# The way back from the experts: pairs of 64-column float32 products from one unsplit buffer

## The chip, the cores and the metric

The kernel runs on one core of a Trainium2 chip. The metric is the time of one execution on the device in microseconds (us); the kernel before takes 1039.68 us, the median of 3 runs (1038.59 to 1040.19).

## The reference

A decoder trunk of two layers on 512 tokens of 1024 features, all in float32. Each layer is a mixer and then a hierarchical mixture of experts, both with a residual and a layer norm. The mixture is what the change touches:

```python
def hier_moe(x, rg_w, rg_b, re_w, re_b, w1, w3, w2):
    ...   # top-1 of 4 groups, then top-2 of the group's 8 experts: gates (tokens, 32), zero for experts not chosen
    def expert(acc, params):
        w1e, w3e, w2e, ge = params
        h = jax.nn.silu(xf @ w1e) * (xf @ w3e)
        return acc + ge[:, None] * (h @ w2e), None
    out, _ = lax.scan(expert, jnp.zeros_like(xf), (w1, w3, w2, gates.T.astype(x.dtype)))
    return out.reshape(B, S, D)
...
    x = layer_norm(ALPHA * x + mixer(x))      # per layer, with its gain and offset
    x = layer_norm(ALPHA * x + hier_moe(x))
```

So each token's row of the result is its own row plus the gated outputs of two experts.

## The kernel before

The program has four parts in a row: mixer of layer 0, its mixture, mixer of layer 1, its mixture (`trunk_kernel`). The rows of `x` lie in four tiles of 128 tokens with 1024 features each (`x_63` to `x_66` in the lists below).

**The mixture** (`moe`) never computes an expert for a token that did not choose it. The routing gives each expert a list of places. Fourteen groups of 128 places are worked off one after the other: the first four hold two experts of 64 places each, the other ten are put together of blocks of 32 places, so that a group is one, two, three or four experts wide (tile sizes 128, 64, 32 columns in the shapes of the profile). For a group, GpSimd gathers the 128 rows from memory (`xg`), TensorE transposes them (`pt`) and ScalarE brings them back with gain and offset (`xt`), TensorE multiplies with w1 and w3 (`hidden`, into `ph`, line L1835), ScalarE and VectorE make silu, gate and product (`hs`), TensorE transposes that (`pth`), ScalarE copies it (`hT`), and TensorE multiplies with w2 in two halves of 512 features (`outputs`, into `py`, L1857). Each expert of a group takes its own columns of the array, and writes its own partitions of the bank.

**The way back.** `outputs` does not keep the group's result as it is: `split` (L287, L288) has ScalarE round it to float32r (`yh`) and VectorE make the float32r rest (`yl`). `places` has VectorE make a matrix P of zeros and ones that tells for each of the 128 places which of the 512 tokens it belongs to. `combine` then, for one tile of 128 tokens and one half of the features, multiplies 128 columns of P with `yh` and with `yl`, both into one bank (`pcm`, L1872), and VectorE adds the bank to `x` (L1874). Eight such sums bring a group home. They are not made at once: they go to a list (`todo`), and during the next group `some` takes them from it at fixed places: two before the fourth and two before the last of the eight steps of `hidden`, one between the two halves of the transposes, one after them, and one before each half of `outputs`.

**The order** in the mixture is that of the program: within it no scheduler moves anything. Each engine works down its own list, and waits where an operand is not there.

**The last group.** In layer 0 the sums of the last group are made in the mixer that follows (`sums` in `mixer1`): there `join` normalises each tile of tokens (VectorE: mean; ScalarE: squares with their sum; GpSimd: power -1/2; VectorE: scale), `turn` transposes it in quarters of the features, and `dense` multiplies. In layer 1 the last two groups are summed in `finish`, which also normalises and writes the result. Both lie behind a branch for blocks that found no place (`tc.If`), which is not taken here.

**The planner** (`Flow`). Both mixers are streams of steps; `Flow.run` puts them into one order before the program runs, taking for each step when its operands are expected and when its engine is free. `Flow.cost` has the prices: of a matmul of n columns n/2330 us where the left side is not float32, n/600 us where it is and the product is not narrow (128 rows deep is not). `Flow.clocked` doubles that where the array is expected to be slow. The planner takes the products of TensorE one after the other. The order that comes out is fixed in the program.

Of the kernel before, what the change touches and what calls it, by code (L numbers as in the profile page):

```python
# [30 lines left out]
class Flow:  # L31
    """Puts the work of several streams into one order. A stream is a generator that yields, before each step, the engine
    the step starts on and the tiles it needs; the order follows from when those are expected to be there, with
    `streams` in order of priority."""
# [83 lines left out]
    def enter(self, tensor):  # L118
        """the place of a tile in its ring"""
        ring = self.rings.setdefault(tensor.tag, [])  # L120
        if tensor.name not in self.place:
            self.place[tensor.name] = len(ring)
            ring.append(tensor.name)
        return self.place[tensor.name], ring
# [3 lines left out]
    def is_warm(self, k):  # L128
        """the array runs at its full clock in a tick that follows one with enough columns"""
        return k > 0 and self.columns.get(k - 1, 0.0) >= self.enough  # L130
# [24 lines left out]
    def take(self, pool, shape, name, bufs):  # L155
        """a tile of a ring, once the reads of the one before it there have been put in order"""
        taken = self.rooms.setdefault(name, [])
        while len(taken) >= bufs and not taken[-bufs]:
            yield None
        t = pool.tile(shape, F32, name=name, bufs=bufs)  # L160
        self.enter(t.tensor)
        taken.append(False)
        self.version += 1
        return t, (taken, len(taken) - 1)
# [5 lines left out]
    def run(self, streams):  # L170
# [3 lines left out]
        while state:  # L174
            best, moved = None, False
            # an array that rests is slow: work that fills it first, where there was too little
# [32 lines left out]
def run_streams(main, fill, ratio):  # L209
    """Emit several streams of work in one order. A step of a stream yields (tensor-engine time, time from its end until  # L210
    the stream's next step can start), or "blocked" where another stream has to go first. `main` streams go in order of
    priority; `fill` streams take the time in which they wait, and at least `ratio` of theirs."""
# [37 lines left out]
class Kernel:  # L250
# [12 lines left out]
    def setup(self):  # L263
# [12 lines left out]
        # x^T of a mixer; after its projections what the mixture of experts starts with  # L276
        self.xp = self.ctx.enter_context(self.tc.tile_pool(name="xp", bufs=1))
        self.dp = self.ctx.enter_context(self.tc.tile_pool(name="dp", bufs=1, space=DRAM))

    def x_room(self, order=(0, 1, 2, 3)):  # L280
        """x^T: [high, low parts][half of the features]"""
# [9 lines left out]
    def mixer0(self):  # L291
        """Feature-major tiles hold two heads on the partitions and 512 tokens; token-major ones hold two chunks of 64 tokens
        (p = 0, 1) on the partitions, and 4 pairs of chunks, heads and features along them. With L the part of a chunk's
        own tokens, T = (I - L)^-1, W = T a and u0 = T (a k^T v), the state after a chunk is
        decay (S + b^T (W S + u0) + k^T v), so all but the product with S is made for every chunk at once."""
# [6 lines left out]
        with ctx:  # L302
# [19 lines left out]
            # weights in the order of their use  # L322
            # (numbers: columns of the input projection; else rows of the output projection: whose, which, a half of the columns)
# [18 lines left out]
            def halve(raw, eng, e):  # L342
                """the float32r part of weights, and the rest"""
# [22 lines left out]
            # lnx_g for tokens on partitions  # L366
# [55 lines left out]
            def unit(parts):  # L422
                """one bank's worth of products: parts [(left, right)] for every 128 rows"""
# [16 lines left out]
            def dense():  # L440
                """the input projection and the output projection"""
# [20 lines left out]
            def evacuate():  # L462
                n, begun = -1, set()
                for job in jobs:
# [17 lines left out]
                    if ti >= 14:  # L482
                        # u, after zeros for the windows
# [25 lines left out]
            def product(needs, shape, f, e):  # L509
                """a bank with f's products, as soon as engine e can read it"""  # L510
# [9 lines left out]
            def head_sums(src):  # L520
                """sums over the features of each head, token-major"""
# [80 lines left out]
            def within(ps, lhsT, rhs):  # L602
                """products of token-major tiles, chunk by chunk"""
# [4 lines left out]
            def across(ps, lhsT, rhs, out="p", **kw):  # L608
                """products over one half of the partitions that go to either half, a bank for every half"""
# [17 lines left out]
            def solve():  # L627
                """T, transposed, and what follows from it"""
                for i in range(4):
# [56 lines left out]
                    # W and u0  # L686
# [14 lines left out]
                    # what the state is multiplied with, for the next state and for y  # L701
# [12 lines left out]
                    # what chunks add to the state  # L714
# [19 lines left out]
            def side():  # L734
                """what the inverse doesn't wait for: tiles turned token-major, and products with k"""
# [64 lines left out]
            def states():  # L800
                """chunk after chunk: the state, and y"""
                for i in range(4):
# [8 lines left out]
                    # one accumulation for a bank: the first matmul of each half clears it  # L811
# [24 lines left out]
                    # (a state made after the products above goes first, so that these don't run beside them)  # L836
# [12 lines left out]
            def heads():  # L849
                """head norm, bonus and gate"""  # L850
# [87 lines left out]
    def mixer1(self):  # L938
# [5 lines left out]
        with ctx:  # L944
# [12 lines left out]
            # weights in the order of their use: (what, which), [rows / 128, columns]  # L957
# [68 lines left out]
            def sums():  # L1026
                """the last of the sums of the mixture before; the sums of every tile go to its layer norm"""
                for t in range(NT):
                    total[t] = bp.tile([128, 2], F32, name=f"jsum{t}", bufs=1)
                    for h in range(2):  # L1030
                        fs = slice(512 * h, 512 * h + 512)
                        ps, room = yield from bank(pp, [512], "pp")
                        ops = [(P, y) for P, ys in late for y in ys]
                        for n, (P, y) in enumerate(ops):
                            yield "PE", (P, y)
                            mm(ps, P[:, 128 * t:128 * t + 128], y[:, fs], start=n == 0, stop=n == len(ops) - 1)
# [6 lines left out]
            def join(t):  # L1043
                """layer norm of the mixture before; x gets its gain and offset later"""
# [13 lines left out]
            def turn(h, g):  # L1058
                """x^T of a quarter of the features of two tiles of tokens, with gain and offset"""
# [343 lines left out]
    def moments(self, pool, x):  # L1403
        """mean, and the reciprocal of the standard deviation"""
# [17 lines left out]
    def start(self, L, flow, pool, turn, sums):  # L1422
        """streams for the start of the mixture: what it takes from memory (once the room of x^T is free), then for every
        tile of tokens the logits and the normalised rows. The router takes x as it is: gain, offset, mean and deviation
        go into its weights, and into what becomes of its sums."""
# [96 lines left out]
    def moe(self, L, last):  # L1522
        """The first experts have 64 places each, two to a group of 128, and their weights are there before the routing is
        known. The others follow in the order of their tokens, places as `limits` has it: a block of 32, and one more for each
        limit their rank is below. What doesn't fit goes to further blocks of 32."""
# [6 lines left out]
        # of every group: whose columns  # L1532
# [18 lines left out]
        with ctx:  # L1551
# [31 lines left out]
            def load(p, known, to=32):  # L1583
                """weights in the order of their use, as far as there is room after the group p"""
# [41 lines left out]
            # routing  # L1626
# [9 lines left out]
            def ranked(src, n, tag):  # L1636
                """how many of the n are ahead: greater, or as great and earlier"""
# [7 lines left out]
            def gated(to, engine):  # L1645
                """weights that are to come behind what the engine does now"""
# [22 lines left out]
            # place of every assignment in its expert's list  # L1669
# [10 lines left out]
            # of the first experts, which are a group: which assignments are theirs, and the tokens  # L1680
# [15 lines left out]
            def chosen(dst, src, n=32):  # L1696
                """of every assignment its expert's entry"""
# [24 lines left out]
            def tokens(name, tab, n):  # L1722
                """the token of every slot, for the gather (out of bounds where there is none) and as a number"""
# [18 lines left out]
            for h in range(2):  # L1742
                # of the first group the halves of the features by themselves
# [8 lines left out]
            # gates, in three parts that bfloat16 holds  # L1752
# [39 lines left out]
            # ranks of the other experts by how many tokens they have, and who has which  # L1792
# [18 lines left out]
            def columns(xrows, xt=None, halves=(0, 1), both=False):  # L1811
                """x^T of 128 slots"""
# [16 lines left out]
            def hidden(xt, ws, gate, beside=(), now=False):  # L1829
                """gate silu(x w1) (x w3), 128 slots shared by some experts"""  # L1830
# [19 lines left out]
            def outputs(hT, ws, y=None):  # L1850
                yh, yl = y or [bp.tile([128, D], F32R, name=n, bufs=3) for n in ("yh", "yl")]
                for half in range(2):
# [5 lines left out]
                    self.split(yh[:, h], yl[:, h], ps)  # L1858
                return yh, yl

            def places(tok, P=None):
                if P is None:
                    P = bp.tile([128, S], F32R, name="P", bufs=3)
# [3 lines left out]
            def combine(parts, t, half, scale, total=None, room=None):  # L1867
                """x <- scale x + the rows of ys, each at its token; its sum"""
                ps = (room or pr).tile([128, 512], F32, name="pcm", tag="py" if room else "pr")
                ops = [(P, y) for P, ys in parts for y in ys]  # L1870
                for n, (P, y) in enumerate(ops):
# [324 lines left out]
```

## Time and profile before

| | |
|---|---|
| median of 3 runs | 1039.68 us (1038.59 to 1040.19) |
| profiled execution, first to last instruction (its span; the page has no other time of it) | 1034.8 us |
| TensorE matmuls (PE) busy | 914.6 us, 88% |
| VectorE (DVE) busy | 734.7 us, 71% |
| ScalarE (ACT) busy | 339.5 us, 33% |
| GpSimd (POOL) busy | 327.5 us, 32% |
| mean granted clock of TensorE | 0.933 of full speed |

An engine's time is that between start and end of its instructions. Matmuls overlap: the next starts before the one ahead has drained, so the durations of single matmuls add up to more than the time they take, and the distance from start to start is what one costs in a row. A float32 matmul is two records on TensorE, a float32r matmul one. The experts' matmuls lie between about 337 and 509 us and between 836 and 1020 us of the span.

### The profile page before, as it was taken

Reading aid. Unit: us, or ns where it says so; the run is one execution under the profiler, and the core shown is the slowest. Engines: PE = TensorE matmul, PEld = TensorE weight load, DVE = VectorE, ACT = ScalarE, POOL = GpSimd, SP = SyncE. Lnnn points to the kernel's source line nnn. Section 1 sums busy time; section 2 is a strip of 40 time slices with the busy share of each in tenths; the row PEclk is TensorE's granted clock in tenths of the full one; section 3 lists DMA queues with packets and bytes.
Section 4 is the critical chain, followed back from the end, with each engine's and each line's share of the span. In section 5 each row is a group of like instructions: output and inputs, shape, how many; then the busy total and the mean of one; then the engine's idle time right before and its main releaser. Section 6 shows DMA issues by size and latency. Waiting matters only on the chain. (4 is left out here: it accounts for less than half of the span.)

```text
span 1034.8 us, 18665 instructions
## 1 busy us (share of the span) xinstructions
PE 914.6 (88%) x7364; PEld 644.3 (62%) x7364; DVE 734.7 (71%) x1527; ACT 339.5 (33%) x690; POOL 327.5 (32%) x298
## 2 busy tenths in 40 slices
PE   6999999999995599999879589779999748999993
PEld 5777777777775255545368568778878624545542
DVE  3565868576777977776676999994733698767666
ACT  3543242433214233433353012212502333433333
POOL 2120414135303810100169446663422281100003
PEclk9999999999997799999989789988888969999997
DMA  7210101011176859788152121221325165976742
GB/s 216 82 43 22 43 24 41 24 43 60 43 280 221 307 225 359 274 345 334 42 161 76 47 81 42 82 82 41 116 102 214 62 246 227 347 282 247 306 197 83
DMA packets 60012, 156.97 MB, mean 152 GB/s; under 512 B 5153, under 2 KB 40097, under 8 KB 51728
## 3 DMA queue, kind: packets, MB, share of 16 engines
q1 hardware_dynamic: 54256, 141.79, 37.4%
q0 software_dynamic: 4512, 9.74, 3.0%
q10 hardware_dynamic: 1152, 4.19, 1.0%
q8 instruction: 60, 0.98, 0.4%
q14 instruction: 32, 0.26, 0.1%
HBM read 155.71 MB, written 6.29 MB: 157 GB/s over the span
## 5 line engine op out<-in xcount | busy, mean ns | idle before, releaser
L1874 DVE SCALAR_TENSOR_TENSOR x<-x,pcm 128x512 f32<-128x512 f32 x210 | 137.0, 683 | 54.5 <-PE pcm L1872 54.2
L57 PE MATMUL pp<-x,wh 128*128 128x512 f32 x480 | 163.5, 423 | 6.4 <-DVE u L57 5.1
L57 PE MATMUL pp<-wh,x 128*128 128x256 f32 (+1 forms) x544 | 139.2, 342 | 23.3 <-DVE u L57 11.4
L57 DVE SCALAR_TENSOR_TENSOR acc<-u,cw,acc 128x512 f32<-128x512 f32 x120 | 127.8, 1120 | 0.7
L57 ACT CAST wh<-wr 128x512 fp32r<-128x512 f32 (+1 forms) x82 | 61.8, 776 | 192.5 <-PE pp L57 129.0
L57 PEld LDWEIGHTS pp<-wh,x 128*128 128x128 f32 x544 | 100.2, 209 | 34.6 <-DVE u L57 11.6
L1835 PE MATMUL ph<-we,xt 128*64 128x256 f32 (+1 forms) x928 | 116.8, 389 | 0.0
L57 PEld LDWEIGHTS pp<-x,wh 128*128 128x128 f32 x480 | 85.9, 195 | 29.0 <-issue 6.2
L1872 PE MATMUL pcm<-yh,P 128*128 128x512 f32 x216 | 99.2, 459 | 3.0 <-DVEq L2043 2.3
L57 PE MATMUL pp<-x,wl 128*128 128x512 f32 x240 | 96.3, 401 | 0.0
L57 POOL TENSOR_TENSOR wl<-wr,wh 128x1024 fp32r<-128x1024 f32 x28 | 83.3, 2988 | 34.5 <-ACT wh L57 34.5
L57 PE MATMUL pp<-wl,x 128*128 128x256 f32 (+1 forms) x272 | 91.1, 335 | 0.0
L1872 PE MATMUL pcm<-yl,P 128*128 128x512 f32 x216 | 85.8, 397 | 5.1 <-DVE yl L288 5.1
L1824 ACT ACTIVATE xt<-pt,x 128x128 f32<-128x128 f32 x224 | 84.8, 471 | 15.6 <-PE pt L1818 15.6
L1835 PEld LDWEIGHTS ph<-we,xt 128*64 128x64 f32 (+1 forms) x928 | 56.8, 129 | 47.1 <-issue 31.7
L1738 POOL DMA_INDIRECT xg<-xd,imx x20 | 19.9, 993 | 191.9 <-PE pt L1818 147.3
L1872 PEld LDWEIGHTS pcm<-yh,P 128*128 128x128 f32 x216 | 40.6, 188 | 52.0 <-DVE x L1874 28.7
L57 DVE SCALAR_TENSOR_TENSOR x<-x,pp 128x512 f32<-128x512 f32 x64 | 43.6, 685 | 39.6 <-PE pp L57 39.5
L1857 PE MATMUL py<-we,hT 128*64 128x512 f32 (+1 forms) x232 | 62.8, 628 | 0.4 <-ACT hT L1847 0.4
L288 DVE TENSOR_TENSOR yl<-py,yh 128x512 fp32r<-128x512 f32 x54 | 37.1, 691 | 34.3 <-ACT yh L287 34.3
L1839 ACT ACTIVATE hs<-ph 128x128 f32<-128x128 f32 x28 | 7.8, 277 | 160.0 <-PE ph L1835 160.0
L57 PEld LDWEIGHTS pp<-wl,x 128*128 128x128 f32 x272 | 57.4, 211 | 2.8
(427 smaller groups left out, 1657.7 us busy)
## 6 DMA issues: line engine op xcount, KB each, us to landing
we<-in_c_experts_dram SPq DMA_DIRECT2D x56, 1536.0 KB, 9.5
wr<-in_ev_w_in_dram SPq DMA_DIRECT2D x18, 512.0 KB, 3.9
x<-in_c_experts_dram SPq DMA_DIRECT2D x8, 1024.0 KB, 6.1
wr<-in_od_w_in_dram SPq DMA_DIRECT2D x7, 1024.0 KB, 5.1
wr<-in_ev_w_out_dram SPq DMA_DIRECT2D x8, 512.0 KB, 3.7
x<-in_c_experts_dram SPq DMA_DIRECT2D x8, 512.0 KB, 4.2
xd<-x ACTq DMA_DIRECT2D x8, 512.0 KB, 4.1
wr<-in_od_w_in_dram SPq DMA_DIRECT2D x8, 512.0 KB, 5.7
```

The costliest lines, as they stand in the source:

```text
L57: r = f(*args, **kw)
L288: (eng or nc.vector).tensor_tensor(lo, src, hi.bitcast(F32), op=OP.subtract)
L1738: G.indirect_dma_start(out=xg[n % NG], out_offset=None, in_=xd, in_offset=bass.IndirectOffsetOnAxis(ap=idx, axis=0), bounds_check=S - 1, o ...
L1824: A.activation(xt[:, kk], ps[:, k], AF.Identity, scale=gc[:, kk:kk + 1], bias=bc[:, kk:kk + 1])
L1835: mm(hp[r], xt[:, k, r], w[0][:, k], start=k == 0, stop=k == KT - 1)
L1839: A.activation(hs, hp[:, 0], AF.Silu)
L1857: mm(ps[r], hT[:, r], w[1][:, h], start=True, stop=True)
L1872: mm(ps, P[:, 128 * t:128 * t + 128], y[:, 512 * half:512 * half + 512], start=n == 0, stop=n == len(ops) - 1)
L1874: V.scalar_tensor_tensor(xs, xs, scale, ps, op0=OP.mult, op1=OP.add, accum_out=total)
```

## The change

`outputs` keeps the group's result in one float32 buffer `y`, by the same copy of ScalarE; VectorE's part of the split is gone. P is float32. A new function `paired` makes of one product two, each with 64 of the 128 columns of P, into the two halves of the bank; `combine` and `sums` call it once per group where they called the plain product twice. The scratch tile of `finish` takes the new buffer's room. Comments and docstrings are dropped as well, and lines shift by some six.

```diff
+    @staticmethod
+    def paired(mm, out, lhsT, rhs, **kw):
+
+        for c in (slice(0, 64), slice(64, 128)):
+            mm(out[c], lhsT[:, c], rhs, **kw)
...
                         ps, room = yield from bank(pp, [512], "pp")
-                        ops = [(P, y) for P, ys in late for y in ys]
-                        for n, (P, y) in enumerate(ops):
+                        for n, (P, y) in enumerate(late):
                             yield "PE", (P, y)
-                            mm(ps, P[:, 128 * t:128 * t + 128], y[:, fs], start=n == 0, stop=n == len(ops) - 1)
+                            self.paired(mm, ps, P[:, 128 * t:128 * t + 128], y[:, fs], start=n == 0, stop=n == len(late) - 1)
...
             def outputs(hT, ws, y=None):
-                yh, yl = y or [bp.tile([128, D], F32R, name=n, bufs=3) for n in ("yh", "yl")]
+                if y is None:
+                    y = bp.tile([128, D], F32, name="y", bufs=3)
                 for half in range(2):
...
-                    self.split(yh[:, h], yl[:, h], ps)
-                return yh, yl
+                    A.copy(y[:, h], ps)
+                return y
 
             def places(tok, P=None):
                 if P is None:
-                    P = bp.tile([128, S], F32R, name="P", bufs=3)
+                    P = bp.tile([128, S], F32, name="P", bufs=3)
...
-                ops = [(P, y) for P, ys in parts for y in ys]
-                for n, (P, y) in enumerate(ops):
-                    mm(ps, P[:, 128 * t:128 * t + 128], y[:, 512 * half:512 * half + 512], start=n == 0, stop=n == len(ops) - 1)
+                for n, (P, y) in enumerate(parts):
+                    self.paired(mm, ps, P[:, 128 * t:128 * t + 128], y[:, 512 * half:512 * half + 512], start=n == 0,
+                                stop=n == len(parts) - 1)
...
-                    y = self.xp.tile([128, 2, D], F32R, name="x1")
-                    y = y[:, 0], y[:, 1]
-                    P = self.xp.tile([128, 4, S], F32R, name="x2")[:, 0]
+
+                    y = self.xp.tile([128, 2, D], F32, name="x1")[:, 0]
+                    P = self.xp.tile([128, 4, S], F32, name="x2")[:, 0]
...
-                junk = bp.tile([128, D], F32R, name="yl", bufs=3)
+                junk = bp.tile([128, D], F32, name="y", bufs=3)
```

**In a group of two experts** TensorE's list keeps its places and changes what stands in them. Its rows between the last step of `hidden` and the second half of `outputs` are before:

```order
L1835 MATMUL ph<-we,xt 64x256 x2
L1818 MATMUL pt<-ident,xg_3880 128x128 x4
L1872 MATMUL pcm<-yh,P 128x512
L1872 MATMUL pcm<-yl,P 128x512
L1845 MATMUL pth<-ident,hs 128x128
L1818 MATMUL pt<-ident,xg_3880 128x128 x4
L1872 MATMUL pcm<-yh,P 128x512
L1872 MATMUL pcm<-yl,P 128x512
L1872 MATMUL pcm<-yh,P 128x512
L1872 MATMUL pcm<-yl,P 128x512
L1857 MATMUL py<-we,hT 64x512 x2
```

and now:

```order
L1840 MATMUL ph<-we,xt 64x256 x2
L1823 MATMUL pt<-ident,xg_3880 128x128 x4
L284 MATMUL pcm<-y,P 64x512 x2
L1850 MATMUL pth<-ident,hs 128x128
L1823 MATMUL pt<-ident,xg_3880 128x128 x4
L284 MATMUL pcm<-y,P 64x512 x4
L1863 MATMUL py<-we,hT 64x512 x2
L284 MATMUL pcm<-y,P 64x512 x2
```

Each pair of 128-column products (`yh`, `yl`) has become a pair of 64-column products of `y`; a row with x4 is two sums.

**At the entry to the second mixer** the planner puts the work into another order. On VectorE the sums of the four tiles (`jsum`), their means (`jnm`) and their normalisations (which read `jrs`) stood so before:

```order
L57 SCALAR_TENSOR_TENSOR x_63,jsum_6050<-x_63,pp 128x512 x2
L57 SCALAR_TENSOR_TENSOR jnm_6068<-jsum_6050,mean 128x1
L57 SCALAR_TENSOR_TENSOR x_64,jsum_6066<-x_64,pp 128x512 x2
L57 SCALAR_TENSOR_TENSOR x_65,jsum_6080<-x_65,pp 128x512
L57 SCALAR_TENSOR_TENSOR jnm_6082<-jsum_6066,mean 128x1
L57 SCALAR_TENSOR_TENSOR x_65,jsum_6080<-x_65,pp 128x512
L57 SCALAR_TENSOR_TENSOR x_66,jsum_6097<-x_66,pp 128x512
L57 SCALAR_TENSOR_TENSOR jnm_6099<-jsum_6080,mean 128x1
L57 SCALAR_TENSOR_TENSOR x_66,jsum_6097<-x_66,pp 128x512
L57 SCALAR_TENSOR_TENSOR jnm_6111<-jsum_6097,mean 128x1
L57 TENSOR_SCALAR x_63<-x_63,jnm_6068,jrs_6070 128x1024
L57 TENSOR_SCALAR x_64<-x_64,jnm_6082,jrs_6084 128x1024
```

and now:

```order
L57 SCALAR_TENSOR_TENSOR x_63,jsum_6006<-x_63,pp 128x512 x2
L57 SCALAR_TENSOR_TENSOR jnm_6028<-jsum_6006,mean 128x1
L57 TENSOR_SCALAR x_63<-x_63,jnm_6028,jrs_6030 128x1024
L57 SCALAR_TENSOR_TENSOR x_64,jsum_6026<-x_64,pp 128x512 x2
L57 SCALAR_TENSOR_TENSOR jnm_6045<-jsum_6026,mean 128x1
L57 TENSOR_SCALAR x_64<-x_64,jnm_6045,jrs_6047 128x1024
L57 SCALAR_TENSOR_TENSOR x_65,jsum_6043<-x_65,pp 128x512 x2
L57 SCALAR_TENSOR_TENSOR jnm_6071<-jsum_6043,mean 128x1
L57 TENSOR_SCALAR x_65<-x_65,jnm_6071,jrs_6073 128x1024
L57 TENSOR_TENSOR x_5990<-xf,x_5988 128x2x256
L57 SCALAR_TENSOR_TENSOR x_66,jsum_6069<-x_66,pp 128x512 x2
L57 SCALAR_TENSOR_TENSOR jnm_6095<-jsum_6069,mean 128x1
```

The normalisation of a tile, which waits for GpSimd's `jrs`, has moved ahead of the sums of the next tile.

On TensorE, at the end of the transposes of the third and fourth tile of tokens (`x_65`, `x_66`), with the kernel of the convolution (`cwr`) and the first products of the projection, there stood before:

```order
L57 MATMUL pt<-ident,x_65 128x128 x2
L57 MATMUL pt<-ident,x_66 128x128 x2
L57 MATMUL ps<-ident,x_65 128x128 x2
L57 MATMUL ps<-ident,x_66 128x128 x2
L57 MATMUL pt<-ident,cwr 128x31 x4
L57 MATMUL pp<-wh,x_6032 128x256
L57 MATMUL pp<-wl,x_6032 128x256
L57 MATMUL pp<-wh,x_6034 128x256
```

and now:

```order
L57 MATMUL pt<-ident,x_66 128x128 x2
L57 MATMUL ps<-ident,x_66 128x128 x2
L57 MATMUL pt<-ident,cwr 128x31 x4
L57 MATMUL pp<-wh,x_5988 128x256
L57 MATMUL pp<-wl,x_5988 128x256
L57 MATMUL pp<-wh,x_5990 128x256
L57 MATMUL pp<-wh,x_5988 128x256
L57 MATMUL pp<-wl,x_5988 128x256
L57 MATMUL pp<-wh,x_5990 128x256
L57 MATMUL pt<-ident,x_66 128x128 x2
L57 MATMUL ps<-ident,x_65 128x128 x2
L57 MATMUL ps<-ident,x_66 128x128 x2
```

The first two of the eight steps of the projection (three products each) now stand ahead of the last transposes of these two tiles.

## Rows read from the trace of the kernel before

**Rows 1.** Stage sums: length; busy us PE, PEld, DVE, ACT, POOL (instructions); clock, DMA share, GB/s.
```profile
358.30:508.10 149.80, 146.92 (x966) 76.82 (x965) 105.99 (x207) 54.31 (x147) 10.47 (x11) 1.00 0.71 274
...
856.80:1005.10 148.30, 145.21 (x940) 75.47 (x941) 101.62 (x205) 53.33 (x144) 10.51 (x11) 1.00 0.71 276
```

**Rows 2.** Timeline, TensorE, one group: start us, duration us, engine, line, names, shapes, count.
```profile
463.90 1.47 PE L1835 MATMUL ph<-we,xt 128*64 128x256 f32 x12
465.29 0.50 PE L1872 MATMUL pcm<-yh,P 128*128 128x512 f32 x1
465.63 0.39 PE L1872 MATMUL pcm<-yl,P 128*128 128x512 f32 x1
465.86 0.40 PE L1872 MATMUL pcm<-yh,P 128*128 128x512 f32 x1
...
466.42 1.95 PE L1835 MATMUL ph<-we,xt 128*64 128x256 f32 x16
...
469.42 0.65 PE L1835 MATMUL ph<-we,xt 128*64 128x256 f32 x4
470.01 0.66 PE L1818 MATMUL pt<-ident,xg 128*128 128x128 f32 x4
470.42 0.48 PE L1872 MATMUL pcm<-yh,P 128*128 128x512 f32 x1
...
470.97 0.27 PE L1845 MATMUL pth<-ident,hs 128*128 128x128 f32 x1
...
471.44 0.48 PE L1872 MATMUL pcm<-yh,P 128*128 128x512 f32 x1
...
472.58 1.08 PE L1857 MATMUL py<-we,hT 128*64 128x512 f32 x4
473.59 0.50 PE L1872 MATMUL pcm<-yh,P 128*128 128x512 f32 x1
...
474.25 1.08 PE L1857 MATMUL py<-we,hT 128*64 128x512 f32 x4
475.16 0.38 PE L1835 MATMUL ph<-x,xt 128*64 128x256 f32 x1
```

**Rows 3.** Timeline, TensorE, the group with a single expert.
```profile
894.70 0.58 PE L1872 MATMUL pcm<-yh,P 128*128 128x512 f32 x1
895.11 0.39 PE L1872 MATMUL pcm<-yl,P 128*128 128x512 f32 x1
```

**Rows 4.** The page's costliest groups: the split on VectorE (busy us, mean ns).
```profile
L288 DVE TENSOR_TENSOR yl<-py,yh 128x512 fp32r<-128x512 f32 x54 | 37.1, 691 | 34.3 <-ACT yh L287 34.3
```

**Rows 5.** Waits of TensorE in the two stretches: us, times, longest.
```profile
PE pcm L1872 <- DVE yl L288: 2.4, 1, 2.4
...
PE pcm L1872 <- DVE yl L288: 2.7, 1, 2.7
```

**Rows 6.** Timeline of the end: the first product and the last add of `finish`.
```profile
1013.25 0.47 PE L1872 MATMUL pcm<-yh,P 128*128 128x512 f32 x1 [2.35 <-DVEq L2043]
...
1023.92 0.68 DVE L1874 SCALAR_TENSOR_TENSOR x<-x,pcm 128x512 f32<-128x512 f32 x1
```

**Rows 7.** Timeline of the entry to the second mixer, 511 to 538 us.
```profile
511.78 1.15 PE L57 MATMUL pp<-x,x 128*128 128x512 f32 x4 [2.64 <-DVEq L2043]
...
513.00 4.71 POOL L57 TENSOR_TENSOR wl<-x,wh 128x1024 fp32r<-128x1024 f32 x2 [1.16 <-ACT wh L57]
...
517.85 1.15 ACT L57 ACTIVATE qkv<-x,jnm 128x1024 f32<-128x1024 f32 x1 [1.18 <-DVE jnm L57]
518.08 0.57 POOL L57 TENSOR_TENSOR jrs<-jrs,nhalf 128x1 f32<-128x1 f32 x1
...
518.95 0.21 DVE L57 SCALAR_TENSOR_TENSOR jnm<-jsum,mean 128x1 f32<-128x1 f32 x1
...
523.26 0.81 DVE L57 TENSOR_SCALAR x<-x,jnm,jrs 128x1024 f32<-128x1024 f32 x1 [0.44 <-POOL jrs L57]
...
537.15 0.36 PE L57 MATMUL pp<-wh,x 128*128 128x256 f32 x1 [2.42 <-DVE rot L57]
```

## Prediction

> **What bounds the kernel now.** I read the stage sums first, then the matmul timeline of one group of experts, then the waits, and last the timelines of the two places where the two layers' mixtures of experts end. The stage sums [rows 1] say where the changed work lies: in two stretches, 149.8 us and 148.3 us long, TensorE is busy for 146.9 and 145.2 us at a granted clock of 1.00, while VectorE is busy for 106.0 and 101.6 us and the DMA engines for 0.71 of their time. So in both stretches TensorE is the bound, and what lengthens its work lengthens the kernel. A part of a group's matmuls can be read as the distance from its start to the start of the next piece, since the durations shown overlap. In one group of two experts [rows 2] the expert products and the way-back products follow one another without a hole from 463.90 to 475.16: 11.26 us. Weights, gathers and the drains on ScalarE and VectorE lie beside it.
>
> **What a sum costs now.** For each tile of 128 tokens and half of the features (I call that a sum) TensorE makes two float32r products, high and low part. In steady flow such a product takes 0.23 us (465.63 to 465.86), the first after an expert product 0.34 [rows 2]. A group has eight sums in blocks of 2, 2, 1, 2 and 1. Start to start: 465.29 to 466.42 is 1.13 (the second block of two is like it), 470.42 to 470.97 is 0.55, 471.44 to 472.58 is 1.14, 473.59 to 474.25 is 0.66. Together 1.13 + 1.13 + 0.55 + 1.14 + 0.66 = 4.61 us for eight sums.
>
> **What a sum will cost.** The new pair has the very shape of an expert's last product: two float32 products, each of 128 rows by 64 columns, with 512 moving columns, into the two halves of one bank. The trace has that pair as four records (each float32 product is two): 0.91 us from 474.25 to 475.16, and 1.01 from 472.58 to 473.59, where the array changes over to a 128-column product [rows 2]. The same products with 256 moving columns, in sixteens and twelves, run at 1.39/12 = 0.116 us a record with the changeover at the end, so without it a little under 0.11, or 0.43 for a pair of 256 columns; a pair of 512 is then 0.86. I take 0.86 inside a block, with 1.01 as the upper end. Eight sums: 6.88 us, +2.27 over 4.61. Around them changeovers move. Gone are those on the expert products' side: 0.1 at the end of the twelve, of the sixteen and of the first output pair and 0.05 at the start of four pieces that follow sums, 0.5 in all. New ones come at three places where sums meet transposes, which are 128 columns wide: 0.15 each, by the 0.58 that four records take between a sum and a transpose where 0.43 would do; 0.45 in all. Net +2.2 us a group. The lower end, with the new changeovers free, is +1.8; the upper, all eight pairs at 1.01, is 8.08 - 4.61 = +3.5.
>
> The rows say that not all of a changeover is one of width: in the group whose single expert fills all 128 columns the first float32r product still takes 0.41 (894.70 to 895.11), against 0.34 and 0.23 above [rows 2, 3], with no change of width before it. The Trainium skill (TensorEngine Tiling (Array Packing), Key Properties) has only the width: changing the tiling mode drains the engine. By that rule the three new changeovers are paid and the sum stays as above; if it is mostly the number format that costs, they are nearly free, 0.3 to 0.45 a group less, and the time would be some 10 us lower.
>
> **The whole of both mixtures.** 27 of the 28 groups are summed in `combine`, 27 x 8 = 216 parts, and the eight of layer 0's last group in the second mixer. 25 groups have a full set of eight beside matmuls (13 in layer 0, 12 in layer 1): 25 x 2.2 = +55. Five places are dearer, since the old changeovers stay: three groups of four 32-column experts and the last of layer 0, by two blocks x 0.3 and two output pairs x 0.15 = 0.9 each, 0.6 for the last, and the single-expert group, where four more blocks now change width, about +1.5. I take +5.
>
> **What goes.** VectorE's split (54 x 0.69 = 37.1 us [rows 4]) lies beside TensorE's work in these stretches and frees nothing there but two waits: 2.4 and 2.7 us, in which the first sum of each layer stands for its low part behind the routing's work on VectorE [rows 5]. ScalarE's copy stays, with the same 128x512 drain. After it nothing else is late: the next user of a bank is 1.7 us of pairs away and VectorE's own add takes 0.68. At the two branches that close the mixtures VectorE no longer finishes a split 0.69 us after ScalarE's copy: 2 x 0.7 = 1.4. Sum: -6.5.
>
> **The end.** In `finish` TensorE makes 14 sum-parts in a row, from 1013.25 on, and VectorE, which adds, normalises and scales, is the bound: its last add starts at 1023.92 [rows 6]. After: 14 x 0.86 = 12.0 us. Starting 0.7 us earlier, that ends at 1024.6, with the last add 0.35 later at 1024.9: +1.0 against before, and with the 0.7 already counted above, +1.7.
>
> **The entry to the second mixer.** Here the order moves, not only the price. The planner takes a new product of 512 columns at 0.85 us and lays the two of a pair one behind the other, so the sums look 3.9 times as dear as before in its clock, and VectorE now gets the normalisation of each tile before the sums of the next (second order fence). In the trace, with the first sum at 511.78 as zero, the first tile's deviation cannot be ready before GpSimd ends the weights' low parts (513.00 + 4.71 = 517.71); the power then runs from 518.08 for 0.57, and the normalisation takes 0.81 [rows 7], so that one ends near +7.7. Before, the adds of the other tiles ran in that time, and the last normalisation ended at 523.26 + 0.81, +12.3. Now tile 1 starts only at +7.7: two adds of 0.68 [rows 6], the mean 0.21, ScalarE's squares 1.15, on GpSimd 0.37 to the power and 0.57 for it, the normalisation 0.81 [rows 7]: 4.47, by my estimate 4.8 with hand-offs. Three such in a row, the last with 0.8 of other work between, end near +23. That is 10.7 later. The weights' product that needs all of it waited until 537.15 [rows 7]; VectorE works down the same list behind it. TensorE's order gets only two of eight steps of the first projection ahead of the last tile. I take +9, between 0 (all of it hidden) and +10.7. From there to the taps of the convolution TensorE is busy throughout and the taps occupy VectorE next, so nothing gives it back.
>
> **The sum** is made against the profiled execution, span 1034.8 us; the page states no other time of it, so I carry the 4.9 us by which the median of the runs, 1039.68, stands above it. 55 + 5 - 6.5 + 1.7 + 9 = +64.2: 1104 us.
>
> **Rivals.**
> - *The entry hides its slip* (+55.2, 1095). For it: in the old entry TensorE idles too, the 2.42 us before 537.15 among that. Against: the new VectorE order is a chain in which each tile waits for GpSimd.
> - *Dear pairs* (1134): every pair at 1.01, so 8 x 0.15 x 25 = +30 on the forecast. For it: 1.01 stands in the rows. Against: only in front of a 128-column product, and inside a block there is none.
> - *Pairs that do not overlap*, so that the change doesn't do what it says: each half then takes the 0.86 of a whole pair, +0.86 x 224 = +193, 1297 us. For it: both halves stream the same rows of `y`, which no pair in the trace does. Against: the output pairs share a bank and a left-hand tile and overlap.
> - *VectorE's relief decides* (the other side, faster): if TensorE in these stretches only looks busy because the ends are modelled, and the queue of sums really moves at VectorE's pace, the longer products fit into its waits, and the 6.5 us of waits go: 1033. It would decide where VectorE's adds and splits end last. Against: VectorE has 44 us of idle time in the first stretch, and its adds wait for TensorE.
>
> **Chances and range.** Forecast 0.62; hidden entry 0.20; dear pairs 0.09; no overlap 0.05; relief 0.03; the rest, about even, 0.01. From 0.2% (2 us), about what a measurement of this kernel can tell from no change, the chances are: faster 0.03, same 0.01, slower 0.96. The unknowns of the forecast itself are a group at +1.8 (-10) and the entry between 0 and +10.7 (-9, +2), against pairs that are 0.05 dearer than 0.86 (25 x 8 x 0.05 = +10) and a further 5 us for the slow clock in a longer entry. That gives 1086 to 1120, with the hidden entry inside it.
>
> **What would show it.** In the profile after: a sum in a block at 0.86 us, four records; groups of two experts every 13.4 us instead of 11.26, without holes on TensorE; no wait for a low part; the fourth normalisation 23 us after the first sum of the second mixer and the projection's wait moved by 9 us; the last add about 11.6 us after the final sums begin. Wrong it is if groups stay at 11.3 (relief) or go to 18 (no overlap), or if VectorE's order at the entry costs nothing.

## The result, and the profile after

The changed kernel takes 1111.97 us (median of 3 runs, 1109.94 to 1116.09) against 1039.68: the ratio is 1.070, 95% interval 1.067 to 1.074. The forecast was 1104 in a range of 1086 to 1120. Direction and range held; 8 us were missing.

The stage sums of the two mixtures, cut from the start of each one's third group to the start of its last (columns as in [rows 1], which are cut elsewhere): first the kernel before, then the changed kernel.

```profile
371.02:497.80 126.78, 126.62 (x821) 66.99 (x817) 90.19 (x172) 48.76 (x132) 9.93 (x10) 1.00 0.80 307
869.77:1002.55 132.78, 132.40 (x861) 68.88 (x858) 90.36 (x174) 48.87 (x132) 9.93 (x10) 1.00 0.75 292
```

```profile
369.71:522.94 153.23, 153.23 (x998) 65.76 (x994) 79.77 (x150) 50.68 (x132) 9.93 (x10) 1.00 0.68 254
919.61:1082.55 162.94, 162.94 (x1038) 65.59 (x1034) 80.07 (x152) 50.71 (x132) 9.90 (x10) 1.00 0.63 238
```

The same groups take 26.45 and 30.16 us more. By the profile TensorE is busy for the whole of both windows, at a granted clock of 1.00 as before; VectorE's share has fallen from 71% (90.19 of 126.78) to 52% (79.77 of 153.23). The bound is the one it was.

One group of two experts in the changed kernel, TensorE's timeline (start, duration, line, names, records), against [rows 2]:

```profile
481.97 1.47 PE L1840 MATMUL ph<-we,xt 128*64 128x256 f32 x12
483.26 1.89 PE L284 MATMUL pcm<-y,P 128*64 128x512 f32 x8
484.98 1.90 PE L1840 MATMUL ph<-we,xt 128*64 128x256 f32 x16
...
488.95 0.66 PE L1823 MATMUL pt<-ident,xg 128*128 128x128 f32 x4
489.54 1.08 PE L284 MATMUL pcm<-y,P 128*64 128x512 f32 x4
490.55 0.33 PE L1850 MATMUL pth<-ident,hs 128*128 128x128 f32 x1
...
493.01 1.03 PE L1863 MATMUL py<-we,hT 128*64 128x512 f32 x4
493.87 1.03 PE L284 MATMUL pcm<-y,P 128*64 128x512 f32 x4
494.73 1.03 PE L1863 MATMUL py<-we,hT 128*64 128x512 f32 x4
495.59 0.38 PE L1840 MATMUL ph<-x,xt 128*64 128x256 f32 x1
```

Read from start to start: two sums take 483.26 to 484.98, 1.72, so a pair costs 0.86. The twelve records of `hidden` ahead of them and the output pair at 493.01 have lost their changeovers (1.29 and 0.86, against 1.39 and 1.01 before). The sum between transposes takes 489.54 to 490.55, 1.01: a changeover has moved there. The group lasts 481.97 to 495.59, 13.62 us instead of 11.26; the forecast was 13.4.

The entry to the second mixer in the changed kernel, VectorE's four normalisations, against [rows 7]; the first sum is at 539.39:

```profile
547.39 0.81 DVE L57 TENSOR_SCALAR x<-x,jnm,jrs 128x1024 f32<-128x1024 f32 x1 [2.25 <-POOL jrs L57]
...
551.99 0.81 DVE L57 TENSOR_SCALAR x<-x,jnm,jrs 128x1024 f32<-128x1024 f32 x1 [2.31 <-POOL jrs L57]
...
557.12 0.82 DVE L57 TENSOR_SCALAR x<-x,jnm,jrs 128x1024 f32<-128x1024 f32 x1 [2.75 <-POOL jrs L57]
...
562.30 1.75 DVE L57 TENSOR_SCALAR x<-x,jnm,jrs 128x1024 f32<-128x1024 f32 x1 [1.40 <-POOL jrs L57]
```

They stand 4.6, 5.1 and 5.2 us apart (I had 4.8), each behind a wait for GpSimd: the chain of the forecast. The last ends 24.7 us after the first sum; 23 was said.

Laid on one another stretch by stretch, the profiled executions give the table (us against before; the two last columns are experiments below, in which an unused tile gives the pool its old size and, in the last, the entry its old order). The spans differ by more (+79.5) than the medians (+72.3): the profiled execution of the changed kernel is the slowest of its three (1116.09), and that of the kernel before lies by my estimate some 3 us under its median (the span plus the 1.8 us by which the time exceeds the span in the other runs is 1036.6). The forecast's terms are sorted by place: 13 x 2.2 + 0.9 + 0.6 - 2.4 - 0.7 in layer 0, 12 x 2.2 + 2 x 0.9 + 1.5 - 2.7 - 0.7 in layer 1; its round +5 makes the sum 64.0 here for 64.2.

| stretch | forecast | changed | room back | room and old order |
|---|---|---|---|---|
| up to layer 0's first expert product | 0 | -0.6 | -0.7 | +0.5 |
| from there to the second mixer's first sum | +27.0 | +28.2 | +29.0 | +27.1 |
| from there to layer 1's first expert product | +9.0 | +19.6 | +8.8 | +3.5 |
| from there to the first of the final sums | +26.3 | +31.6 | +27.9 | +28.0 |
| from there to the end | +1.7 | +0.7 | +1.0 | +0.7 |
| span (before: 1034.8) | +64.0 | +79.5 | +66.0 | +59.7 |

The excess lies in two rows, on either side of layer 1's first expert product. There the weights of layer 1 are loaded. First the kernel before, then the changed one: a wait of SyncE's queue ahead of these loads, and its timeline.

```profile
SPq L1568 <- DVE rn L57: 22.5, 1, 22.5
```

```profile
767.67 2.19 SPq L1568 DMA_DIRECT2D we<-in_c_experts_dram  x4
...
779.93 0.33 SPq L1610 DMA_DIRECT2D x<-in_ln_mix_g_dram  x1
```

```profile
SPq L1573 <- DVE x L57: 79.9, 1, 79.9
```

```profile
862.98 2.21 SPq L1573 DMA_DIRECT2D we<-in_c_experts_dram  x4
...
865.94 0.49 SPq L1615 DMA_DIRECT2D x<-in_ln_mix_g_dram  x1
```

Before, four weight loads (1.5 MB each) wait 22.5 us for an instruction of VectorE in the mixer (`rn`) and go out at 767.67, 68 us ahead of the first expert product; the gain row follows at 779.93. After, the first load waits 79.9 us for VectorE's last work on the mixer's output (`x`), and all of them start at 863, just ahead of the gathers of token rows. What that does, in the changed kernel's timelines of GpSimd, TensorE and VectorE:

```profile
871.82 1.15 POOL L1749 DMA_INDIRECT xg<-xd,ixh  x1 [10.14 <-DVE gb L1777]
...
887.44 2.34 POOL L1985 TENSOR_TENSOR x<-x,x 128x1024 f32<-128x1024 f32 x1 [9.83 <-DMA x<-in_ln_mix_g_dram]
...
895.86 2.40 POOL L1986 TENSOR_TENSOR x<-x,x 128x1024 f32<-128x1024 f32 x1
898.23 2.35 POOL L1985 TENSOR_TENSOR x<-x,x 128x1024 f32<-128x1024 f32 x1
```

```profile
879.34 1.09 PE L1823 MATMUL pt<-ident,xg 128*128 128x128 f32 x4 [11.19 <-DMA xg<-xd,ixh]
882.20 1.11 PE L1823 MATMUL pt<-ident,xg 128*128 128x128 f32 x4 [1.77 <-DMA xg<-xd,ixh]
...
909.03 3.59 PE L284 MATMUL pcm<-y,P 128*64 128x512 f32 x8 [10.14 <-DVE x L1880]
```

```profile
893.26 2.56 DVE L1890 TENSOR_SCALAR pq<-pi 128x8 int32<-128x8 int32 x1
...
895.96 2.33 DVE L1895 SCALAR_TENSOR_TENSOR pc<-po,pc 128x8 f32<-128x8 f32 x1
898.22 0.15 DVE L1896 SCALAR_TENSOR_TENSOR pb<-po,pb 128x8 f32<-128x8 f32 x1
898.33 2.28 DVE L1895 SCALAR_TENSOR_TENSOR pc<-po,pc 128x8 f32<-128x8 f32 x1
```

The gathers now run beside the weights: from 863 to 884 us the DMA engines are busy for 0.95 of the time (0.24 in the 20 us up to the same product in the kernel before), and the transposes wait 11.19 and 1.77 us for the gathers (4.13 and 0.34 before). The gain row comes late too, so GpSimd's products with it start at 887.44 and lie beside VectorE's plan for the blocks (the routing's work from `pq` on). There instructions of eight elements take 2.3 us or 0.15. The long ones end with the instruction of GpSimd that runs beside them (895.96 + 2.33 = 898.29, and 895.86 + 2.40 = 898.26); the short one shown stands where GpSimd goes from one to the next. The first add stands behind that plan, and TensorE waits 10.14 us for a bank.

Why the load waits is in the pools. The low and high parts took 2 x 3 buffers of 4 KB a partition, the one float32 tile takes 3: 12 KB less. The pool of the weight buffers is opened next in the program, so they begin 12 KB lower, on rooms that the mixer still uses.

### The profile page after: what moved, and what is told of

Read it like the earlier page. It is cut to its first block, busy times and chain, and to the rows that moved or that the text cites. A ratio compares the mean times of both kernels' runs of the same rounds, so it can differ in the third digit from the quotient of the medians.

```text
span 1114.3 us, 19502 instructions
## 1 busy us (share of the span) xinstructions
PE 990.2 (89%) x7812; PEld 635.2 (57%) x7812; DVE 705.2 (63%) x1472; ACT 343.8 (31%) x690; POOL 324.3 (29%) x297
## 5 line engine op out<-in xcount | busy, mean ns | idle before, releaser
L1880 DVE SCALAR_TENSOR_TENSOR x<-x,pcm 128x512 f32<-128x512 f32 x210 | 144.2, 688 | 173.1 <-PE pcm L284 172.9
L284 PE MATMUL pcm<-y,P 128*64 128x512 f32 x864 | 212.3, 605 | 10.6 <-DVE x L1880 10.1
L284 PEld LDWEIGHTS pcm<-y,P 128*64 128x64 f32 x864 | 56.8, 137 | 97.5 <-issue 69.9
L1840 PEld LDWEIGHTS ph<-we,xt 128*64 128x64 f32 (+1 forms) x928 | 60.8, 129 | 56.9 <-issue 42.3
L1863 PE MATMUL py<-we,hT 128*64 128x512 f32 (+1 forms) x232 | 59.0, 605 | 0.4 <-ACT hT L1852 0.4
L1823 PE MATMUL pt<-ident,xg 128*128 128x128 f32 x224 | 37.5, 293 | 17.4 <-DMA xg<-xd,ixh 17.3
L57 PEld LDWEIGHTS pp<-x,wl 128*128 128x128 f32 x240 | 46.5, 194 | 10.9 <-DVE wl L57 0.4
```

What stands on the lines that cost most here:

```text
L57: r = f(*args, **kw)
L284: mm(out[c], lhsT[:, c], rhs, **kw)
L1823: nc.tensor.transpose(ps[:, k], xrows[:, 128 * kk:128 * kk + 128], self.ident)
L1840: mm(hp[r], xt[:, k, r], w[0][:, k], start=k == 0, stop=k == KT - 1)
L1863: mm(ps[r], hT[:, r], w[1][:, h], start=True, stop=True)
L1880: V.scalar_tensor_tensor(xs, xs, scale, ps, op0=OP.mult, op1=OP.add, accum_out=total)
```

## Experiments

Each of the eight kernels was timed beside the kernel before, in five rounds; ratios are against that, and stretches come from each kernel's own profile.

**The changed kernel again.** No edit.

> The changed kernel once more, as the measure for the three beside it. If the loss is in its order and in its rooms, as the trace says, it comes out near 1112 us again and the second layer's first expert product again stands some 8 us further behind the end of its mixer than before. If those 8 us were a chance of the one profiled execution (it was the longest of three), they are gone from this profile and the median is nearer to 1104.

1114.02 us, ratio 1.073 (1.071 to 1.075). Layer 1's first expert product again comes 342.95 us after the second mixer's first sum (343.85 in the first profile, 324.28 before). The excess is no chance of one execution.

**The room back.** An unused tile where the parts had lain:

```diff
                     y = bp.tile([128, D], F32, name="y", bufs=3)
+                    if not hasattr(self, f"room{L}"):
+                        setattr(self, f"room{L}", bp.tile([128, D], F32, name="room", bufs=3))
```

> Only 12 KB a partition of unused room are added where the low parts lay, so that the weight buffers of layer 1 lie where they lay before the change. Theory: in the changed kernel those buffers reach down onto rooms that the mixer's last normalisation still reads, so four weight loads and the gain rows go out at 863 instead of 768 us, beside the gathers; that costs 8.5 us at the first expert product, and GpSimd's late work with the gain rows then holds VectorE and the first sum for some 2.7 us more. With the room back: 1112 - 8.5 - 2.7, about 1101 us (1098 to 1104), the loads at about 770 us of the span. Rival: the gathers are late because everything before them moved by 39 us into other transfers; then the room changes nothing and the time stays at 1112.

1101.31 us, ratio 1.061 (1.059 to 1.064): 12.7 less than the changed kernel beside it. SyncE's wait and timeline in this kernel, and TensorE's wait for the gathers:

```profile
SPq L1573 <- DVE rn L57: 24.9, 1, 24.9
```

```profile
806.28 2.10 SPq L1573 DMA_DIRECT2D we<-in_c_experts_dram  x4
```

```profile
PE pt L1823 <- DMA xg<-xd,ixh: 4.6, 2, 4.3
```

The loads go out at 806.28, not at 770 as I wrote: 38.6 us later than before, about what layer 0 and the entry had lost by then. They wait for `rn` again, as in the kernel before, so they are in their old place. The wait for the gathers is 4.6 us (4.5 before), and the first two groups of layer 1 take 32.68 us (36.37 in the changed kernel, 33.70 before). Nothing computed has changed; 12 KB of address cost 12.7 us.

**The old order at the entry.** The planner takes the new products at the old price, which gives the old order on VectorE, ScalarE and GpSimd:

```diff
...
+            if ins[0].dtype == F32 and ins[0].tensor.name in Flow.cheap:
+                return n / 2330
...
-        passes = 1 if op == "transpose" or lhs.dtype != F32 else 2
+        passes = 1 if op == "transpose" or lhs.dtype != F32 or lhs.tensor.name in Flow.cheap else 2
...
+                            Flow.cheap.add(P.tensor.name)
                             yield "PE", (P, y)
...
```

> The room as in e1, and the planner of the second mixer takes the new products at the old price, so its order is that of the kernel before on VectorE, ScalarE and GpSimd. Theory of the prediction (entry +9): about 10 us less than e1, 1091 (1088 to 1094), the fourth normalisation ending some 12 to 14 us after the first sum instead of 23.7. Rival (the slip is hidden by what follows, so only the place of the wait changes): within 2 us of e1.

1095.71 us, ratio 1.055 (1.053 to 1.057): 5.6 less than with the room alone, not 10. The chain is gone: the fourth normalisation ends 13.6 us after the first sum. From the first sum to layer 1's first expert product it takes 3.5 us more than before. So of the entry's 8.8 us, 5.3 were the order; I had named the whole +9 as one of order, and neither theory had the size.

The 3.5 left over are not shown to come from the change. Three kernels below (no split, rows on VectorE, tile by tile) have the second mixer of the kernel before in the same order, and take 327.45, 324.88 and 327.61 us for this stretch, where the profile before has 324.28 and this kernel 327.76. So the same mixer already differs by 3.3 us from one profile to another.

**One product of 128 columns a sum**, on top of both:

```diff
-        for c in (slice(0, 64), slice(64, 128)):
-            mm(out[c], lhsT[:, c], rhs, **kw)
+        mm(out, lhsT, rhs, **kw)
...
```

> As e2, but each sum is one float32 product of all 128 columns instead of a pair of 64. If the two halves of a pair overlap fully, the sum keeps its price: 0.86 us in two records of 0.43. Changeovers then move back: 0.5 a group returns at the expert products, 0.54 goes at the transposes. Theory that the width of the products makes a changeover: a group at 13.6 us and the time within 2 us of e2. Theory that the number format made them, so that between float32 products of any width there is next to none: a group at 13.1 and some 12 us less than e2. If pairs overlapped only in part, the single product would be under 0.86 and the time lower still.

1105.24 us, ratio 1.065 (1.063 to 1.067): 9.5 more than with pairs. Part of a group of this kernel on TensorE:

```profile
489.74 1.47 PE L1844 MATMUL ph<-we,xt 128*64 128x256 f32 x12
491.13 1.98 PE L287 MATMUL pcm<-y,P 128*128 128x512 f32 x4
493.05 1.95 PE L1844 MATMUL ph<-we,xt 128*64 128x256 f32 x16
...
497.91 1.02 PE L287 MATMUL pcm<-y,P 128*128 128x512 f32 x2
498.77 0.27 PE L1854 MATMUL pth<-ident,hs 128*128 128x128 f32 x1
```

Where no width changes, one wide product takes 497.91 to 498.77, 0.86 in two records: a pair's price, so the halves of a pair overlap fully. But two sums beside the narrow expert products take 491.13 to 493.05, 1.92 instead of 1.72. A group lasts 14.37 against 13.62, and it has eight changes of width against four: 0.75 / 4 = 0.19 us each. All products here are float32, so this is width alone. None of the three theories said slower; I had set the changeovers gone (0.5) against those new (0.45) as if they were alike in number, and they are seven against three.

The group with a single expert is the second witness. Its first product and the first of the next group, before, in the changed kernel and in this one:

```profile
893.48 1.56 PE L1835 MATMUL ph<-x,xt 128*128 128x256 f32 x6
...
903.67 0.64 PE L1835 MATMUL ph<-we,xt 128*32 128x256 f32 x8
```

```profile
947.94 1.56 PE L1840 MATMUL ph<-x,xt 128*128 128x256 f32 x6
...
962.85 0.42 PE L1840 MATMUL ph<-we,xt 128*32 128x256 f32 x4
```

```profile
939.25 1.56 PE L1844 MATMUL ph<-x,xt 128*128 128x256 f32 x6
940.65 1.88 PE L287 MATMUL pcm<-y,P 128*128 128x512 f32 x4
...
952.47 0.85 PE L1844 MATMUL ph<-we,xt 128*32 128x256 f32 x12
```

It lasts 10.19, 14.91 and 13.22 us. With pairs it has ten changes of width, with the wide product none: (14.91 - 13.22) / 10 = 0.17 us each.

**No split on VectorE**, in the kernel before:

```diff
...
-                    self.split(yh[:, h], yl[:, h], ps)
+                    A.copy(yh[:, h], ps)
```

> The kernel before with its two float32r products a sum, but without VectorE's split: the low part is a tile of zeros, written once, so each sum is that of the high parts alone and TensorE does the same work. This weighs the prediction's term for what goes (-6.5 us) by itself: 2.4 and 2.7 us of waits at the first sums and 0.7 at each branch. Theory: 1038.5 - 6.5, about 1032 us (1029 to 1035), a group of two experts still at 11.3. Rival (VectorE's relief decides): groups get shorter, since 37 us less lie on VectorE, and the time falls to 1020 or less. Other rival: VectorE's remaining work before the first adds ends as late as before, and the time stays within 2 us.

1033.61 us, ratio 0.994 (0.992 to 0.996): -5.6, where -6.5 was the term. The first sums still wait 1.4 and 1.6 us here, for the tile of zeros from GpSimd, so the term may be somewhat larger. In the steady flow a group of two experts lasts what it did, 11.25 to 11.40 us; only one, in layer 1, falls from 12.01 to 11.35. What VectorE's 37 us of splits cost lies mostly in the first two groups of each layer, which get 1.5 and 1.8 us shorter; the rival that lets VectorE decide is out.

**The gain and offset rows on VectorE**, in the kernel before:

```diff
-                e = V if t in () else G
+                e = V
```

> The kernel before, with GpSimd's eight products and sums with the gain and offset rows of each layer put on VectorE. Theory: while GpSimd works on these (2.35 us each), VectorE's small instructions stand still until one ends (0.75 us becomes 2.8 to 3.1, 0.16 becomes 2.3), some 14 us in each layer's first two groups; on VectorE the eight take about 1.2 us each, 9.6. So some 4 us less in each layer, 1030 us, with no VectorE instruction of the routing over 1 us except the P tile. Rival (the long VectorE instructions have their own cause, such as the memory they read): VectorE's list becomes 9.6 us longer in each layer and the time rises by 5 to 19 us.

1028.96 us, ratio 0.990 (0.987 to 0.992): faster than both kernels. VectorE's timeline at the start of layer 1 in this kernel:

```profile
833.79 0.76 DVE L1804 TENSOR_TENSOR sq<-rank,x 128x576 f32<-128x576 f32 x1
834.59 0.76 DVE L1805 TENSOR_TENSOR sq<-sq,x 128x576 f32<-128x576 f32 x1
...
836.26 1.22 DVE L1979 TENSOR_TENSOR x<-x,x 128x1024 f32<-128x1024 f32 x1
...
848.01 0.16 DVE L1889 SCALAR_TENSOR_TENSOR pc<-po,pc 128x8 f32<-128x8 f32 x1
```

The first of these stood so in the kernel before, beside GpSimd:

```profile
841.80 3.09 DVE L1804 TENSOR_TENSOR sq<-rank,x 128x576 f32<-128x576 f32 x1
```

```profile
841.92 2.35 POOL L1979 TENSOR_TENSOR x<-x,x 128x1024 f32<-128x1024 f32 x1
```

Its 3.09 us are about GpSimd's 2.35 and its own 0.76 in a row. Eight instructions of 1.22 are added to VectorE's list and the list still ends earlier: the first two groups of layer 1 take 29.70 us for 33.70, those of layer 0 29.89 for 33.86.

**The same in the changed kernel.**

> The changed kernel (rooms as it has them) with the same eight on VectorE. In it GpSimd's share starts late in layer 1, since its rows are loaded late, and the first sum there waits 10 us for VectorE. Theory: the wait goes almost, the late gathers stay: the second layer's first two groups take about 31 us instead of 36, layer 0's start gains 4, so 1103 us (1100 to 1107), with the first expert product of layer 1 still some 18 us later against the mixer's end than before. Rival (the wait is due to the late rows themselves, wherever the work is done): the first two groups stay at 36 us and only layer 0 gains, 1109.

1099.73 us, ratio 1.058 (1.056 to 1.060), a little under the range given. The first two groups of layer 1 fall from 36.37 to 28.69 us, while layer 1's first expert product still comes 341.18 us after the second mixer's first sum, 8.1 later than with the room back (333.10). So the 12 KB act in two separate ways: through late gathers, about 8 us, and through GpSimd's late work beside VectorE's plan.

**Tile by tile.** The kernel before with the rows on VectorE, each tile's just ahead of its first add:

```diff
+                if t in plain:
+                    plain.remove(t)
+                    affine(t)
                 xs = x[t][:, 512 * half:512 * half + 512]
...
```

> The kernel before with the gain and offset rows on VectorE as in f2, but tile by tile, each right before the tile's first add instead of all eight ahead of the first split. In f2 TensorE's first sum of each layer waits 6.6 us for its low part behind them. If that wait is what is left to take, the split comes up to 7 us earlier, the adds catch up in the group that follows, and some 2 to 4 us a layer are gained: 1023 us (1020 to 1027). Rival (VectorE's list of the first two groups is the bound, in whatever order): within 2 us of f2, 1029.

1026.18 us, ratio 0.988 (0.986 to 0.990). The first two groups of layer 1 go from 29.70 to 26.83, as expected; yet the intervals of the two ratios overlap, so whether it beats the version above by a measurable amount is open. Both beat the kernel before by about 1%.

## Why the prediction was right, and where it failed

- **What bounds the kernel** held: TensorE, in both stretches. Taking 37 us off VectorE leaves the steady groups of two experts as they were, but for one.
- **The price of a sum** held to the hundredth: 0.86 a pair. A group came to +2.36, not +2.2. The mis-sized term is the changeovers, at 0.17 to 0.19 each by the wide product, not 0.15 (the row that gave it, 469.42 to 470.01, is 0.59 long, not 0.58). With 0.19 a group is 8 x (0.86 - 2 x 0.233) = 3.15 dearer by its sums, less four changes, 0.76: +2.39. The other reading, that the number format costs, does not hold. The single-expert group has ten changes of format and none of width in the kernel before, and neither in the wide one. There it lasts 13.22 us against 10.19, 3.03 more, and the sums alone should make that 3.15, so ten changes of format are worth some 0.12 us together. The 0.41 of its first float32r product, from which that reading came, is made up by the six records ahead of it: 893.48 to 894.70 is 1.22, and 1.40 in the wide kernel (939.25 to 940.65). By the rule of the Trainium skill that I cited (TensorEngine Tiling (Array Packing), Key Properties) changing the mode drains the engine. The runs agree with it in that a change of width has a price and a change of format hardly any; that the price is that of a drain, none of them shows.
- **The dearer places** were right in kind; the single-expert group came to +4.7 (10.19 to 14.91), 1.0 more than the 2.2 + 1.5 allowed for it.
- **What goes** (-6.5) measured -5.6 by itself. In the changed kernel the wait in layer 1 did not go: 2.7 us became 10.1.
- **The entry** (+9) measured +8.8 with the room back, by the chain foreseen. 5.3 of it is the order; the other 3.5 is not shown to come from the change, so the term was too large by up to that much.
- **The end** (+1.7) came to +0.7: the last add starts 12.7 us after the final sums begin (1092.06 to 1104.76), not 11.6, but what follows it is shorter.
- **The step that failed** is "After it nothing else is late". I followed the low part's instructions and waits and never its room. The smaller pool let the weight buffers down onto rooms still in use: +12.7 us by the medians of one comparison. The sum has no term for these loads at all; it counts weights and gathers as lying beside TensorE's work, which they did not at the start of layer 1. With that room back the kernel takes 1101.3, within 3 us of the forecast. The chain of addresses stood in the profile before as a queue that waits 22.5 us for VectorE's `rn` and issues four loads at 767.67, inside the mixer: a wait for a room, on which I should have put a price.
- **Luck** has a part in the numbers. 1112 lies in the range, but the range's upper side was drawn from dearer pairs and a slow clock, not from rooms. And 1101.3 with the room back lies near 1104 in part because errors cancel: the medians there differ by 62.8, the two mixtures cost 29.0 and 27.9 us by the profiles where 27.0 and 26.3 were said, and so, by this estimate, some 5 to 6 us are left for the entry, not 9.

## What to carry to other kernels

A tile that is no longer needed can also move the pools behind it: look at which early loads depended on free rooms, and keep the room if they move. Count changes of tile width on TensorE by number, one price each, before weighing a narrow form against a wide one; in this flow, which TensorE bounds, what VectorE was spared showed almost only at the ends. Where tiny VectorE instructions last as long as GpSimd's beside them, try GpSimd's work on VectorE. And compare a stretch in several executions before its last few microseconds are put down to a change.

## What the runs showed of the hardware

- A change between 64 and 128 columns costs TensorE 0.17 to 0.19 us at a granted clock of 1.00 (with pairs against wide products, both float32); ten changes between float32 and float32r at one width cost some 0.12 us together.
- VectorE's small instructions stand still until an instruction of GpSimd beside them ends: 0.76 us becomes 3.09 for a product of 576 elements, and 0.15 to 0.17 becomes 2.3 for eight. The Trainium skill (SBUF — State Buffer, SBUF: two separate sides) describes an exclusive lock of the pair of ports that the two share; the runs agree, since the long durations go when GpSimd's work goes.
- GpSimd's eight products and sums with the gain and offset rows take 2.35 us each and more on GpSimd, 1.22 on VectorE, so work put on the idle engine cost more time of the busy one than doing it there.
